# A recurrent layer's weight low parts queued behind the last convolution tap, and the last tile's scans behind a low part

## The chip, the core and the metric

The kernel runs on one core of one Trainium2 chip. The core has five engines, each of which works through a queue of its own strictly in order: TensorE (PE, matrix products; PEld is its weight load), VectorE (DVE), ScalarE (ACT), GpSimd (POOL) and SyncE (SP, which here only issues transfers). An instruction that needs the result of another engine waits at the head of its queue, and everything behind it waits too. The metric is the device time of one execution in microseconds (us). The median of the three runs before is 1522.43 us (1521.42 to 1522.82).

## What is computed

The reference is one inference step of two layers on 640 tokens (512 latent tokens on a grid of 8 x 64, and 128 context tokens), model width 1024. Layer 0 mixes tokens by attention, layer 1 by a linear recurrence in both directions; each is followed by a gated feed-forward part. The change lies in layer 1's mixer:

```python
def _lru_mixer(xm, h0, w_in, conv_w, conv_b, w_a, b_a, w_i, b_i, lam, w_out):
    gate, xr = jnp.split(xm @ w_in, 2, axis=-1)
    xc = _centred_depthwise_conv(xr, conv_w, conv_b).astype(jnp.float32)
    ...
    a_f, b_f = _rglru_coeffs(xc, w_a[0], b_a[0], w_i[0], b_i[0], lam[0])
    a_b, b_b = _rglru_coeffs(xc, w_a[1], b_a[1], w_i[1], b_i[1], lam[1])
    hs_f, hT_f = _linear_scan(a_f, b_f, h0[:, 0], reverse=False)
    hs_b, hT_b = _linear_scan(a_b, b_b, h0[:, 1], reverse=True)
    y = (hs_f + hs_b).astype(xm.dtype) * jax.nn.gelu(gate)
    return y @ w_out, jnp.stack([hT_f, hT_b], axis=1)

def _rglru_coeffs(xc, w_a, b_a, w_i, b_i, lam):
    ...
    r = jax.nn.sigmoid(jnp.einsum('btnk,nkj->btnj', xb, w_a).reshape(B, T, D) + b_a)
    i = jax.nn.sigmoid(jnp.einsum('btnk,nkj->btnj', xb, w_i).reshape(B, T, D) + b_i)
    log_a = -LRU_C * r * jax.nn.softplus(-lam.astype(jnp.float32))
    a = jnp.exp(log_a)
    b = jnp.sqrt(-jnp.expm1(2.0 * log_a)) * (i * xc)
```

The convolution has four taps along the tokens.

## The kernel before

Activations lie with the features on the 128 partitions and the tokens along them, so the width of 1024 makes eight tiles, numbered 0 to 7 here. To keep float32 accuracy on the fast product format, every operand is split into a high part (a rounded copy) and a low part (the rest): `x = xhi + xlo`. A product then takes three matrix products, high by high (L221), high by the activations' low part (L222), and the weight's low part by high (L223). A weight tile of 1024 x 128 is loaded by `unit` twice in the recurrent stage: as it is by a transfer from SP's queue (`raw`), and as its high part by a transfer from POOL's queue (`whi`); DVE computes the low part, `wlo = raw - whi` (L182). Each of the three has three buffers.

A tile's products are made in two chunks of columns, 384 and 256 tokens wide, each 8 x 3 products into one bank of PSUM (`mm`, three banks). The recurrent stage has sixteen such weight tiles: for each of the eight feature tiles an input tile (`lru_xr`, the branch that goes into the convolution) and a gate tile (`lru_gate`, the branch that goes through GeLU).

The work of one feature tile f has four parts:
- `lru_a`: ACT makes the first tap and adds the bias (L1253), DVE the other three taps (L1255), giving `xc`. Four gate products of PE follow (L1265, `gp`, two PSUM buffers; two gates by two directions, each one 512 and one 131 columns wide), and ACT's tanh of each (L1266). DVE multiplies the input gate by `xc` (L1267).
- `lru_b`: ACT's two exponentials (L1277) and two tanh (L1278), a square root (L1279), with table loads where its functions change; DVE's L1273 before it, and L1280 and L1281 behind it.
- `lru_c`: DVE's four scans, two directions by latent and context tokens (L1290), POOL's copies of the final states (L1292), DVE's sums of the two directions (L1297, L1298).
- `lru_d`: DVE multiplies by the gate branch (L1302), ACT casts the high part (L1307), DVE makes the low part (L1309). These are the operands of the output projection.

The loop in `run` goes over steps t = 0 to 9 and writes, in step t: `lru_a` of tile t, the input tile of t + 1, `lru_b` of tile t - 1, `lru_c` of tile t - 2, the gate tile of t - 2 (from step 3 on), `lru_d` of tile t - 2. The order in each engine's queue isn't this order, though. A scheduler in the framework plays the program through on a model of the machine at build time and queues each instruction when the model has it ready. `issue_after` (wrapped as `pin`) adds a constraint: what is written inside it may not be queued ahead of a given instruction on that instruction's engine. It is an order, not a wait. `unit` and `halves` have an argument `after` for that, which only the low part's instruction (L182) obeys.

The input branch has two buffers (`xr0`, `xr1`), so tile t + 1 can be written while tile t is read. The output projection (`project_halves`) begins with five chunks that use the operand tiles 0 to 5 only, and closes them with tiles 6 and 7.

Of the kernel before, what the change touches and what calls it, by code (L numbers as in the profile page):

```python
# [9 lines left out]
F32 = mybir.dt.float32  # L10
F32R = mybir.dt.float32r
AF = mybir.ActivationFunctionType
ALU = mybir.AluOpType
# [4 lines left out]
KT = D // P  # L18
# [15 lines left out]
LW = 643  # L34
# [91 lines left out]
class _Step:  # L126
# [1121 lines left out]
    def lru_a(self, f, lp):  # L1248
        nc, xr = self.nc, self.xrs[f % 2]
        gw = self.t([P, 2, 2, P], F32, "gw", 2, lp)  # L1250
        nc.sync.dma_start(gw, self.i["wg"][f])
        xc = self.t([P, LW], F32, "xc", 2, lp)
        nc.scalar.activation(xc, xr[:, 0:LW], AF.Identity, scale=self.col("cw0", f), bias=self.col("cb", f))  # L1253
        for j in range(1, 4):
            nc.vector.scalar_tensor_tensor(xc, xr[:, j:j + LW], self.col(f"cw{j}", f), xc, ALU.mult, ALU.add)  # L1255

        def lt():
            return self.t([P, 2, LW], F32, "lt", NLT, lp)
        tr, ti = lt(), lt()
        for w, tl in enumerate((tr, ti)):  # L1260
            for d in range(2):
                c = (w * 2 + d) * KT + f
                ps = self.pp.tile([P, 1024], F32, tag="gp", name=self.nm("gp"), bufs=2)
                for s0, s1 in ((0, 512), (512, LW)):
                    nc.tensor.matmul(ps[:, s0:s1], gw[:, w, d], xc[:, s0:s1], start=True, stop=True)  # L1265
                nc.scalar.activation(tl[:, d], ps[:, 0:LW], AF.Tanh, scale=0.5, bias=self.hb[:, c:c + 1])  # L1266
        nc.vector.scalar_tensor_tensor(ti, ti, 1.0, xc[:, None, :].broadcast_to([P, 2, LW]), ALU.add, ALU.mult)  # L1267
        return lt, tr, ti
# [14 lines left out]

    def lru_c(self, f, a, h):
        nc = self.nc
        for d in range(2):
            st = self.st[:, d * KT + f:d * KT + f + 1]
            for sl, init in ((slice(0, NLAT), self.col(f"h{d}", f)), (slice(C0, LW), 0.0)):
                hv, av = [t[:, d, sl] if d == 0 else t[:, d, sl][:, ::-1] for t in (h, a)]
                nc.vector.tensor_tensor_scan(hv, av, hv, init, ALU.mult, ALU.add)  # L1290
            e = LW - 1 if d == 0 else C0
            nc.gpsimd.tensor_copy(st, h[:, d, e:e + 1])  # L1292
        y = a[:, 0, 0:NTOK]
        fn, bn = [h[:, d, 0:NLAT].rearrange("p (r c) -> p c r", r=ROWS) for d in range(2)]
        for c0, c1, q0 in ((56, 64, 0), (0, 56, 64)):
            yv = y[:, q0:q0 + (c1 - c0) * ROWS].rearrange("p (c r) -> p c r", r=ROWS)
            nc.vector.tensor_tensor(yv, fn[:, c0:c1], bn[:, c0:c1], ALU.add)  # L1297
        nc.vector.tensor_tensor(y[:, NLAT:NTOK], h[:, 0, C0:LW], h[:, 1, C0:LW], ALU.add)  # L1298
        return y

    def lru_d(self, f, y, G, yhi, ylo):
        self.nc.vector.tensor_tensor(y, y, G, ALU.mult)  # L1302
        self.split(yhi[:, f], ylo[:, f], y)

    def split(self, hi, lo, v, after=(None, None)):
        with self.pin(after[1]):
            self.nc.scalar.copy(hi, v)  # L1307
        with self.pin(after[0]):
            self.nc.vector.tensor_tensor(lo, v, hi.bitcast(F32), ALU.subtract)  # L1309

    def lru_gate(self, f, hi, lo, lp, after=None):
        nc = self.nc
# [19 lines left out]
    def run(self):  # L1332
        nc, tc, i, o = self.nc, self.tc, self.i, self.o
# [19 lines left out]
        xhi = self.big()  # L1353
        xlo = self.big()
# [43 lines left out]
        xhi = self.big(n=NTOK + 2)  # L1398
        xlo = self.big(n=NTOK + 2)
# [12 lines left out]
        xhi, xlo = self.nh, self.nl  # L1412

        yhi = self.big()
        ylo = self.big()
        with self.phase("lru", at=1) as lp:
            A, B, C, G = {}, {}, {}, {}
            self.xrs = [self.t([P, 648], F32, f"xr{j}", 1, lp) for j in range(2)]
            for xr in self.xrs:
                for a, b in ((0, 2), (514, 517), (645, 648)):  # L1420
                    nc.gpsimd.memset(xr[:, a:b], 0.0)

            def gate(g, after=None):
                G[g], halves = self.lru_gate(g, xhi, xlo, lp, after)
                return halves
            x0, g0, x1 = self.lru_xr(0, xhi, xlo), gate(0, self.sq), self.lru_xr(1, xhi, xlo, self.dg)
            x0[0](pins={3: self.at})
            g0[0](pins={0: self.rr})
            for step in (x1[0], x0[1], g0[1]):
                step()  # L1430
            for t in range(KT + 2):
                if t < KT:
                    A[t] = self.lru_a(t, lp)
                if t + 1 < KT:
                    for step in self.lru_xr(t + 1, xhi, xlo) if t else x1[1:]:
                        step()
                if 0 < t <= KT:
                    B[t - 1] = self.lru_b(t - 1, *A.pop(t - 1))
                if t > 1:
                    C[t - 2] = self.lru_c(t - 2, *B.pop(t - 2))  # L1440
                if t > 2:
                    for step in gate(t - 2):
                        step()
                if t > 1:
                    self.lru_d(t - 2, C.pop(t - 2), G.pop(t - 2), yhi, ylo)
            nc.gpsimd.dma_start(o["nh"], self.st)
        x1, x2 = self.big(n=NTOK + 2), self.big(n=NTOK + 2)
# [33 lines left out]
```

## Time and profile before

| what | value |
|---|---|
| median of three runs | 1522.43 us |
| the profiled execution, whole time | 1522.34 us |
| its span in the trace | 1520.6 us |
| mean granted clock of PE | 0.991 |

The page gives the busy time of each engine. In a trace's row the first number is the start, the second the duration, both in us from the start of the span; then the engine, the line of the code, the operation, and the tiles as out<-in with partitions x columns. A bracket gives the time that the engine sat idle just before and what ended that. PE's rows overlap, since products are pipelined: the distance from one start to the next is what a product costs. A row of a window of time gives for each engine its busy time (and the count of instructions), then the clock that was granted to PE as a share of the full one, the busy share of the transfer engines, and GB/s. The recurrent stage lies between about 855 and 1030 us.

### The profile page before, as it was taken

To read this page: it belongs to the slowest core of one execution; us is meant where nothing else is said; L and a number is where in the kernel's file an instruction comes from. 1 tells how busy PE (TensorE), PEld (TensorE's weight loads), DVE (VectorE), ACT (ScalarE), POOL (GpSimd) and SP (SyncE) were. 2 spreads that over 40 slices of the span, in tenths; PEclk is the share of its full clock that TensorE was granted. 3 is DMA by queue.
4 is the path that set the end of the run, shared out by engine and by line. 5 is a ranking of instruction groups with operands and counts; after the bars stand their busy time and mean duration, and the time that the engine had idled before them with its cause. 6 is when DMAs were issued, how large, how long until landed. Compare 5 with 4: busy or idle time off the path is not lost. (4 is left out here: it accounts for less than half of the span.)

```text
span 1520.6 us, 26091 instructions
## 1 busy us (share of the span) xinstructions
PE 1491.0 (98%) x10359; PEld 1443.9 (95%) x10359; DVE 1062.4 (70%) x2005; ACT 697.9 (46%) x1268; POOL 253.2 (17%) x276
## 2 busy tenths in 40 slices
PE   8999999899999999999999999999999999999997
PEld 6999999899999999999999888899999999999997
DVE  5778998769999987434443769985965656566555
ACT  4576666754332123312321478864634342434243
POOL 0112132100111110000000114220322323222211
PEclk9999999999999999999999999999999999999999
DMA  9545665336566664222222443335342231323211
GB/s 379 165 142 162 188 188 172 117 136 187 179 190 197 207 195 134 62 84 84 65 64 92 145 131 109 119 104 175 97 125 83 71 111 56 100 67 98 70 56 70
DMA packets 72330, 196.65 MB, mean 129 GB/s; under 512 B 8048, under 2 KB 24592, under 8 KB 72080
## 3 DMA queue, kind: packets, MB, share of 16 engines
q1 hardware_dynamic: 57392, 142.32, 29.7%
q0 software_dynamic: 14240, 51.98, 11.2%
q8 instruction: 81, 1.33, 0.4%
q10 hardware_dynamic: 576, 0.68, 0.1%
q14 instruction: 41, 0.34, 0.1%
HBM read 179.48 MB, written 8.92 MB: 124 GB/s over the span
## 5 line engine op out<-in xcount | busy, mean ns | idle before, releaser
L221 PE MATMUL mm<-big,whi 128*128 128x320 f32 (+3 forms) x1233 | 383.7, 313 | 6.5 <-ACT big L1307 5.3
L222 PE MATMUL mm<-big,whi 128*128 128x320 f32 (+3 forms) x1233 | 383.7, 312 | 0.4 <-DVE big L564 0.2
L223 PE MATMUL mm<-big,wlo 128*128 128x320 f32 (+3 forms) x1233 | 383.9, 312 | 0.0
L221 PEld LDWEIGHTS mm<-big,whi 128*128 128x128 f32 x1233 | 232.8, 189 | 9.2 <-ACT big L1307 6.0
L222 PEld LDWEIGHTS mm<-big,whi 128*128 128x128 f32 x1233 | 233.3, 189 | 2.8 <-DVE big L1309 0.7
L223 PEld LDWEIGHTS mm<-big,wlo 128*128 128x128 f32 x1233 | 232.9, 189 | 1.5
L250 DVE SCALAR_TENSOR_TENSOR mprod<-mraw,csb 128x1024 f32<-128x1024 f32 x160 | 195.1, 1219 | 12.3 <-DMA mraw<-in_wm 11.8
L587 DVE SCALAR_TENSOR_TENSOR x<-mm,G,x 128x320 f32<-128x320 f32 (+2 forms) x192 | 77.9, 436 | 83.7 <-PE mm L223 83.5
L180 ACT CAST whi<-raw 128x1024 fp32r<-128x1024 f32 (+1 forms) x71 | 73.9, 1041 | 108.6 <-PE mm L222 62.4
L182 DVE TENSOR_TENSOR wlo<-raw,whi 128x1024 fp32r<-128x1024 f32 (+1 forms) x87 | 106.0, 1219 | 21.6 <-ACT whi L180 12.5
L221 PE MATMUL mm<-big,whx 128*128 128x320 f32 (+3 forms) x348 | 108.3, 311 | 0.0
L223 PE MATMUL mm<-big,wlx 128*128 128x320 f32 (+3 forms) x348 | 108.0, 310 | 0.0
L222 PE MATMUL mm<-big,whx 128*128 128x320 f32 (+3 forms) x348 | 107.8, 310 | 0.0
L246 POOL DMA_DIRECT2D mraw<-in_wm x80 | 43.1, 538 | 364.8 <-DVE mprod L250 270.5
L221 PE MATMUL mx<-big,whi 128*128 128x320 f32 (+3 forms) x287 | 89.4, 311 | 0.0
L223 PE MATMUL mx<-big,wlo 128*128 128x320 f32 (+3 forms) x287 | 89.1, 311 | 0.0
L222 PE MATMUL mx<-big,whi 128*128 128x320 f32 (+3 forms) x287 | 88.9, 310 | 0.0
L221 PE MATMUL mx<-big,whx 128*128 128x320 f32 (+3 forms) x260 | 80.6, 310 | 0.0
L223 PE MATMUL mx<-big,wlx 128*128 128x320 f32 (+3 forms) x260 | 80.5, 310 | 0.0
L180 ACT CAST whx<-raw 128x1024 fp32r<-128x1024 f32 (+1 forms) x40 | 41.1, 1029 | 85.5 <-PE mm L222 47.9
L222 PE MATMUL mx<-big,whx 128*128 128x320 f32 (+3 forms) x260 | 80.3, 309 | 0.0
L1307 ACT CAST whi<-raw 128x1024 fp32r<-128x1024 f32 (+1 forms) x41 | 41.3, 1008 | 73.2 <-PE mm L222 44.9
(347 smaller groups left out, 3721.5 us busy)
## 6 DMA issues: line engine op xcount, KB each, us to landing
raw<-in_gu SPq DMA_DIRECT2D x88, 512.0 KB, 3.5
mraw<-in_wm POOLq DMA_DIRECT2D x80, 512.0 KB, 3.9
raw<-in_dn SPq DMA_DIRECT2D x24, 512.0 KB, 3.6
sw<-in_wm SPq DMA_DIRECT2D x16, 512.0 KB, 10.7
raw<-in_wqk SPq DMA_DIRECT2D x16, 512.0 KB, 5.0
raw<-in_wi SPq DMA_DIRECT2D x16, 512.0 KB, 3.6
whi<-in_wi POOLq DMA_DIRECT2D x16, 512.0 KB, 4.1
raw<-in_dn SPq DMA_DIRECT2D x16, 448.0 KB, 3.3
```

The lines of the kernel that those rows point to most:

```text
L180: nc.scalar.copy(hi, raw)
L182: nc.vector.tensor_tensor(lo, raw, hi.bitcast(F32), ALU.subtract)
L221: nc.tensor.matmul(ps, hi[:, k], xhi[:, k, s], start=(k == 0), stop=False)
L222: nc.tensor.matmul(ps, hi[:, k], xlo[:, k, s], start=False, stop=False)
L223: self.done = nc.tensor.matmul(ps, lo[:, k], xhi[:, k, s], start=False, stop=(k == last)).ins
L246: nc.gpsimd.dma_start(w, self.i["wm"][l * 6 + j - 2, f])
L250: nc.vector.scalar_tensor_tensor(prod, w, 1.0, self.csb[:, s], ALU.mult, ALU.mult, accum_out=out[:, s, f:f + 1])
L587: self.nc.vector.scalar_tensor_tensor(xs, ps[:, a - t0:b - t0], G[:, s, f:f + 1], xs, ALU.mult, ALU.add)
L1307: self.nc.scalar.copy(hi, v)
```

## The change

There are two edits. First, `lru_a` keeps its last tap's instruction as `self.conv`, and the input tile of step t (from step 1 on) and the gate tile of step t (steps 3 to 7) are made with it as `after`: their low parts may not be queued ahead of the last tap of tile t. Second, `split` returns the instruction of the low part, `lru_d` keeps it as `self.low`, and the scans of the last tile (f = 7) may not be queued ahead of it; at that point it is the low part of tile 6.

```diff
         for j in range(1, 4):
-            nc.vector.scalar_tensor_tensor(xc, xr[:, j:j + LW], self.col(f"cw{j}", f), xc, ALU.mult, ALU.add)
+            self.conv = nc.vector.scalar_tensor_tensor(xc, xr[:, j:j + LW], self.col(f"cw{j}", f), xc, ALU.mult, ALU.add).ins
...
     def lru_c(self, f, a, h):
         nc = self.nc
+        pin = self.low if f == KT - 1 else None
...
-                nc.vector.tensor_tensor_scan(hv, av, hv, init, ALU.mult, ALU.add)
+                with self.pin(pin):
+                    nc.vector.tensor_tensor_scan(hv, av, hv, init, ALU.mult, ALU.add)
...
     def lru_d(self, f, y, G, yhi, ylo):
         self.nc.vector.tensor_tensor(y, y, G, ALU.mult)
-        self.split(yhi[:, f], ylo[:, f], y)
+        self.low = self.split(yhi[:, f], ylo[:, f], y)
...
-            self.nc.vector.tensor_tensor(lo, v, hi.bitcast(F32), ALU.subtract)
+            return self.nc.vector.tensor_tensor(lo, v, hi.bitcast(F32), ALU.subtract).ins
...
-                    for step in self.lru_xr(t + 1, xhi, xlo) if t else x1[1:]:
+                    for step in self.lru_xr(t + 1, xhi, xlo, self.conv) if t else x1[1:]:
                         step()
...
                 if t > 2:
-                    for step in gate(t - 2):
+                    for step in gate(t - 2, self.conv if t < KT else None):
                         step()
```

Since the scheduler plays the whole program through again, the order moves on all engines in this stage. The rows below are the queues as built, without times; line numbers behind L1255 are higher by two in the changed kernel (the scans, L1290, become L1292; L1297 and L1298 become L1299 and L1300; L1302 becomes L1304; L1309 becomes L1311).

**DVE, from the last tap of tile 1 to that of tile 2.** `xc_1624` is tile 1's convolution, `xc_1638` tile 2's. `lt_1616` and `lt_1617` belong to tile 0, `lt_1625` and `lt_1626` to tile 1. `wlo_1668` and `wlo_1681` are low parts of weight tiles, `wlo_1647` that of step 2's input tile. Before:

```order
L1255 SCALAR_TENSOR_TENSOR xc_1624_9718<-xr1_1598_9503,cols_1_61,xc_1624_9718 128x643
L1273 TENSOR_SCALAR lt_1616_9670<-lt_1616_9670 128x1286
L1267 SCALAR_TENSOR_TENSOR lt_1617_9671<-lt_1617_9671,xc_1615_9665 128x1286
L1255 SCALAR_TENSOR_TENSOR xc_1638_9813<-xr0_1597_9502,cols_1_61,xc_1638_9813 128x643
L182 TENSOR_TENSOR wlo_1668_10026<-raw_1666_10023,whi_1667_10025 128x1024
L1255 SCALAR_TENSOR_TENSOR xc_1638_9813<-xr0_1597_9502,cols_1_61,xc_1638_9813 128x643 x2
```

And now, from L1280 of tile 0 on:

```order
L1280 SCALAR_TENSOR_TENSOR lt_1616_9670<-lt_1636_9802,lt_1616_9670 128x1286
L1255 SCALAR_TENSOR_TENSOR xc_1638_9813<-xr0_1597_9502,cols_1_61,xc_1638_9813 128x643
L1281 TENSOR_TENSOR lt_1617_9671<-lt_1617_9671,lt_1616_9670 128x1286
L1255 SCALAR_TENSOR_TENSOR xc_1638_9813<-xr0_1597_9502,cols_1_61,xc_1638_9813 128x643
L1292 SCALAR_TENSOR_TENSOR lt_1617_9671<-lt_1636_9802,cols_1_61,lt_1617_9671 128x512
L1292 SCALAR_TENSOR_TENSOR lt_1617_9671<-lt_1636_9802,lt_1617_9671 128x128
L1292 SCALAR_TENSOR_TENSOR lt_1617_9671<-lt_1636_9802,cols_1_61,lt_1617_9671 128x512
L1292 SCALAR_TENSOR_TENSOR lt_1617_9671<-lt_1636_9802,lt_1617_9671 128x128
L1255 SCALAR_TENSOR_TENSOR xc_1638_9813<-xr0_1597_9502,cols_1_61,xc_1638_9813 128x643
L182 TENSOR_TENSOR wlo_1647_9840<-raw_1645_9837,whi_1646_9839 128x1024
```

Tile 2's taps moved from ahead of tile 0's L1280, L1281 and scans to between them, and the input tile's low part, which stood ahead of tile 1's taps, now stands behind tile 2's last.

**ACT, ahead of the first tap of tile 2.** `mm_1634` and `mm_1635` are the two chunks of tile 2's input branch, copied into `xr0`. Before, the copies of the second chunk stood behind the last tanh of tile 0, with the tap behind them:

```order
L1266 ACTIVATE lt_1617_9671<-gp_1620_9680,l_hb_388_2009 128x643
L1266 ACTIVATE lt_1617_9671<-gp_1621_9684,l_hb_388_2009 128x643
L1245 COPY xr0_1597_9502<-mm_1635_9775 128x16x8
L1245 COPY xr0_1597_9502<-mm_1635_9775 128x128
L1253 ACTIVATE xc_1638_9813<-xr0_1597_9502,cols_1_61 128x643
```

Now a step's whole chain stands ahead of it:

```order
L1266 ACTIVATE lt_1626_9724<-gp_1629_9733,l_hb_388_2009 128x643
L1277 ACT_TABLE_LOAD
L1277 ACTIVATE lt_1636_9802<-lt_1616_9670,l_sm4_387_2007 128x643 x2
L1245 COPY xr0_1597_9502<-mm_1634_9748 128x8x8
L1245 COPY xr0_1597_9502<-mm_1634_9748 128x40x8
L1278 ACTIVATE lt_1616_9670<-lt_1616_9670,l_sp2_386_2005 128x643 x2
L1266 ACTIVATE lt_1626_9724<-gp_1630_9737,l_hb_388_2009 128x643
L1245 COPY xr0_1597_9502<-mm_1635_9775 128x16x8
L1245 COPY xr0_1597_9502<-mm_1635_9775 128x128
L1279 ACT_TABLE_LOAD
L1279 ACTIVATE lt_1616_9670<-lt_1616_9670 128x1286
L1253 ACTIVATE xc_1638_9813<-xr0_1597_9502,cols_1_61 128x643
```

Tile 2's first tap moved from behind tile 0's tanh to behind tile 1's tanh and tile 0's square root. In the later steps the same chain stands there, one tile further on.

**PE, ahead of the first gate product of tile 2** (`gp_1641`). `mm_1648` and `mm_1649` are the chunks of step 2's input tile (weights `whi_1646`, `wlo_1647`), `mm_1662` the first chunk of step 3's. Before, the input tile of step 2 was done and the next begun:

```order
L223 MATMUL mm_1649_9870<-big_1512_8886,wlo_1647_9840 128x256
L221 MATMUL mm_1662_9950<-big_1512_8886,whi_1660_9946 128x384
L222 MATMUL mm_1662_9950<-big_1513_8887,whi_1660_9946 128x384
L223 MATMUL mm_1662_9950<-big_1512_8886,wlo_1661_9947 128x384
L221 MATMUL mm_1662_9950<-big_1512_8886,whi_1660_9946 128x384
L1265 MATMUL gp_1641_9820<-xc_1638_9813,gw_1637_9811 128x512
```

Now:

```order
L221 MATMUL mm_1649_9870<-big_1512_8886,whi_1646_9839 128x256
L222 MATMUL mm_1649_9870<-big_1513_8887,whi_1646_9839 128x256
L221 MATMUL mm_1662_9950<-big_1512_8886,whi_1660_9946 128x384
L222 MATMUL mm_1662_9950<-big_1513_8887,whi_1660_9946 128x384
L1265 MATMUL gp_1641_9820<-xc_1638_9813,gw_1637_9811 128x512
L1265 MATMUL gp_1641_9820<-xc_1638_9813,gw_1637_9811 128x131
L1265 MATMUL gp_1642_9824<-xc_1638_9813,gw_1637_9811 128x512
L1265 MATMUL gp_1642_9824<-xc_1638_9813,gw_1637_9811 128x131
L223 MATMUL mm_1648_9843<-big_1512_8886,wlo_1647_9840 128x384
```

All but the first pair of each chunk of step 2's input tile moved behind tile 2's first two gate products. The later steps stand alike: first pairs, the step's first two gate products, most of the input tile's first chunk, the other two gate products among its end, its second chunk, and from step 3 on the gate tile.

At the end of the stage DVE's queue had the scans of tiles 6 and 7 in one piece; now a weight's low part, tile 6's sums, its product with the gate branch and its low part stand between them. Tile 7's sums, product and low part follow its scans.

## The prediction

> **What bounds the kernel now.** I read the page first, then the waits, then the recurrent stage (about 855 to 1030 us) in slices and in order of time.
>
> ```profile
> PE 1491.0 (98%) x10359; PEld 1443.9 (95%) x10359; DVE 1062.4 (70%) x2005; ACT 697.9 (46%) x1268; POOL 253.2 (17%) x276
> ```
>
> TensorE (PE) is busy 98% of the span, so the kernel is bound by it, and time can be won or lost only where PE stands still or runs slowly. In the recurrent stage three of its waits exceed 1 us (times in us; row: start, duration, engine, line; in brackets the idle time before it):
>
> ```profile
> 918.17 1.97 PE L1265 MATMUL gp<-xc,gw 128*128 128x512 f32 x4 [1.85 <-ACT lt L1266]
> 978.92 1.32 PE L1265 MATMUL gp<-xc,gw 128*128 128x512 f32 x4 [1.07 <-issue]
> 1020.09 0.41 PE L221 MATMUL mm<-big,whi 128*128 128x320 f32 x1 [1.63 <-ACT big L1307]
> ```
>
> The second is one that the change touches. VectorE (DVE) had this in its queue just then:
>
> ```profile
> 976.80 1.22 DVE L182 TENSOR_TENSOR wlo<-raw,whi 128x1024 fp32r<-128x1024 f32 x1 [2.11 <-DMA whi<-in_wi]
> 977.94 0.88 DVE L1255 SCALAR_TENSOR_TENSOR xc<-xr,cols,xc 128x643 f32<-128x643 f32 x1
> ```
>
> A weight's low part waited 2.11 us for its transfer, with the last tap of tile 7 queued behind it; the tap ended at 977.94 + 0.88 = 978.82, and PE's gate product came 0.1 us later. After the first and third wait PE also runs at half clock (the number before the DMA share is the granted clock):
>
> ```profile
> 919.00:920.00 1.00, 1.00 (x4) 0.51 (x3) 1.00 (x1) 0.00 (x0) 1.00 (x1) 0.50 0.93 377
> 920.00:921.00 1.00, 1.00 (x5) 1.00 (x5) 1.00 (x3) 0.83 (x2) 1.00 (x1) 0.50 0.15 57
> 921.00:922.00 1.00, 1.00 (x3) 0.65 (x3) 1.00 (x2) 1.00 (x2) 1.00 (x1) 0.50 0.00 0
> 1022.00:1024.00 2.00, 2.00 (x9) 2.00 (x9) 2.00 (x2) 1.07 (x2) 0.00 (x0) 0.50 1.00 391
> ```
>
> Three microseconds at 0.50 lose 1.5 us; I charge that to every long wait. So the most that the stage can give back is 1.85 + 1.07 + 1.63 + 2 x 1.5 = 7.6 us.
>
> **The change, part by part.** No instruction is added or removed; only queue places move. The first edit ties the low parts of step t's weights behind the last tap of tile t. In the order before, the low part for the input tile of step 2 stood ahead of the taps of tile 1, and PE worked one tile ahead. Now that low part stands behind the last tap of tile 2, so PE can do only the first pair of products of each open chunk before it needs it. In PE's order the gate products of tile t (L1265), which need that same tap, come right after those pairs. PE therefore stands at the first gate product until the last tap of tile t has ended. Call that moment T(t). The question is what lies between T(t) and T(t+1), and whether PE has work for that long.
>
> PE's durations: one gate product, then a 384-wide and a 256-wide chunk of 24 products.
>
> ```profile
> 882.05 1.24 PE L1265 MATMUL gp<-xc,gw 128*128 128x512 f32 x4
> 883.05 0.36 PE L223 MATMUL mm<-big,wlo 128*128 128x256 f32 x1
> ...
> 990.39 0.34 PE L221 MATMUL mm<-big,whi 128*128 128x384 f32 x1
> 994.61 0.28 PE L221 MATMUL mm<-big,whi 128*128 128x256 f32 x1
> 997.46 0.31 PE L221 MATMUL mx<-big,whi 128*128 128x320 f32 x1
> ```
>
> A gate product takes 1.00 from start to start, the chunks 4.22 (0.176 a product) and 2.85 (0.119), a whole weight tile 7.07. A step of PE has four gate products, one input tile and, from step 3 on, one gate tile: 4.0 + 7.07 + 7.07 = 18.1 us, without the gate tile 11.1.
>
> ScalarE's (ACT) durations, one after the other without a gap:
>
> ```profile
> 893.14 1.28 ACT L1277 ACT_TABLE_LOAD   x1
> 894.43 1.74 ACT L1277 ACTIVATE lt<-lt,l_sm 128x643 f32<-128x643 f32 x2
> 896.08 0.91 ACT L1278 ACTIVATE lt<-lt,l_sp 128x643 f32<-128x643 f32 x1
> 896.89 0.78 ACT L1266 ACTIVATE lt<-gp,l_hb 128x643 f32<-128x643 f32 x1
> 897.57 0.92 ACT L1278 ACTIVATE lt<-lt,l_sp 128x643 f32<-128x643 f32 x1
> 898.39 0.48 ACT L1245 COPY xr<-mm 128x128 f32<-128x128 f32 x2
> 898.78 0.79 ACT L1266 ACTIVATE lt<-gp,l_hb 128x643 f32<-128x643 f32 x1
> 899.58 1.28 ACT L1279 ACT_TABLE_LOAD   x1
> 900.87 1.28 ACT L1279 ACTIVATE lt<-lt 128x1286 f32<-128x1286 f32 x1
> 902.06 0.91 ACT L1253 ACTIVATE xc<-xr,cols 128x643 f32<-128x643 f32 x1
> ...
> 904.97 0.84 ACT L1245 COPY xr<-mm 128x64 f32<-128x64 f32 x2
> ```
>
> And DVE's:
>
> ```profile
> 961.58 1.50 DVE L1280 SCALAR_TENSOR_TENSOR lt<-lt,lt 128x1286 f32<-128x1286 f32 x1
> 962.99 0.88 DVE L1255 SCALAR_TENSOR_TENSOR xc<-xr,cols,xc 128x643 f32<-128x643 f32 x1
> 963.79 0.82 DVE L1302 TENSOR_TENSOR lt<-lt,gl 128x640 f32<-128x640 f32 x1
> 964.53 1.49 DVE L1281 TENSOR_TENSOR lt<-lt,lt 128x1286 f32<-128x1286 f32 x1
> 965.93 1.22 DVE L182 TENSOR_TENSOR wlo<-raw,whi 128x1024 fp32r<-128x1024 f32 x1
> 967.07 0.82 DVE L1309 TENSOR_TENSOR big<-lt,big 128x640 fp32r<-128x640 f32 x1
> 967.81 1.28 DVE L1290 TENSOR_TENSOR_SCAN lt<-lt,cols,lt 128x512 f32<-128x512 f32 x1
> 969.00 0.40 DVE L1290 TENSOR_TENSOR_SCAN lt<-lt,lt 128x128 f32<-128x128 f32 x1
> 969.32 1.26 DVE L1290 TENSOR_TENSOR_SCAN lt<-lt,cols,lt 128x512 f32<-128x512 f32 x1
> 970.50 0.40 DVE L1290 TENSOR_TENSOR_SCAN lt<-lt,lt 128x128 f32<-128x128 f32 x1
> 970.81 1.21 DVE L1297 TENSOR_TENSOR lt<-lt 128x64 f32<-128x64 f32 x2
> ```
>
> From these I walk the new queues. **One loop, T(t) to T(t+1)**, in the order that the three queues now have:
> - PE: 0.1 to start, two gate products 2.0, half clock 1.5, sixteen products of the input tile's 384 half 2.8, the third gate product 1.0, and 0.24 by which its record outlasts its turn: 7.6.
> - ACT, which takes its queue in order: tanh 0.8, two exponentials 1.65, tanh (L1278) 0.81, the fourth gate's tanh 0.68, the copies of the 384 half 0.84, tanh 0.82, copies of the 256 half 0.48, table load 1.29, square root 1.28: 8.65. PE has finished both halves by the time ACT copies them.
> - DVE: L1280 needs that root and stands ahead of the first tap: 1.41, tap 0.80, L1281 1.40, tap 0.80, four scans 3.00, last tap 0.88: 8.3.
>
> Together 24.6 us, against 18.1 of PE work (19.6 with the half clock): PE idles 5 us or more a step, and long waits bring the half clock each time. In steps 4 to 6 ACT loads one more table ahead of the exponentials (1.29), and in step 4 L1302 stands ahead of the last tap (0.74) and two more products are needed first (0.35): 27.0, 25.9, 25.9.
>
> **The start.** PE begins the input tile of step 1 at 872.59; tile 1's first tap follows ACT's row at 873.39.
>
> ```profile
> 868.64 1.81 DVE L1255 SCALAR_TENSOR_TENSOR xc<-xr,cols,xc 128x643 f32<-128x643 f32 x2 [4.87 <-ACT xc L1253]
> ...
> 872.59 0.34 PE L221 MATMUL mm<-big,whi 128*128 128x384 f32 x1
> ...
> 873.39 0.93 ACT L1253 ACTIVATE xc<-xr,cols 128x643 f32<-128x643 f32 x1
> ```
>
> T(0) = 868.64 + 0.80 + 0.80 + 0.88 = 871.1 and T(1) = 874.3 + 2.5 = 876.8 are early enough. PE: pairs until 873.2, two gate products to 875.2, a pair, two more to 877.5, tile 1's first when its bank is emptied, 877.6 to 878.6, 18 products to 881.8, the next gate product to 882.8, three products, and tile 1's third gate product to 884.3. ACT then has 0.8 + 1.29 + 1.65 + 0.84 + 1.64 + 0.68 + 0.48 + 1.29 + 1.28 = 9.95 from 884.5 to the root's end at 894.5; DVE's 8.3 gives T(2) = 902.8. PE has run dry at about 889: 14 us idle. Then T(3) = 927.4, T(4) = 952.0, T(5) = 979.0, T(6) = 1004.9, T(7) = 1030.8, where before T(7) was 978.8: **+52.0 us**.
>
> What gets better is worth little: the low parts no longer hold the taps (the 1.07 above), and PE's other two waits are inside the new ones.
>
> **The tail.** Behind T(7) PE had 1018.46 - 978.92 = 39.5 us of work; now 0.94 of it (three pairs) lies ahead and 1.5 of half clock is added, so it ends at T(7) + 40.2. The second edit puts the scans of tile 7 behind the low part of tile 6. Before, both tiles' high parts came together at T(7) + 41.3. Now tile 6's comes earlier by four scans and a sum (3.0 + 1.2), but the half clock delays the chain by 1.5: T(7) + 38.6, in time. Tile 7's follows after low part 0.8, scans 3.0, sums 1.4 (estimated from the 1.21 row), product 0.8 and cast 0.8 (taken as the rows of the same width): T(7) + 45.4. PE does tile 6's fifteen products meanwhile (2.2, at an estimated 0.147 for 320 columns, between 0.119 and 0.176) and waits. End before: 41.3 + 30 products 4.4 + half clock 1.5 = T(7) + 47.2; now 45.4 + 2.2 + 1.5 = T(7) + 49.1: **+1.9**. Its bounds: -2.2 if tile 7's part came no later than both did before, since PE has then done tile 6's fifteen; +4.6 if tile 6's comes no earlier than before (41.3 + 6.8 + 2.2 + 1.5 = 51.8).
>
> Sum: 52.0 + 1.9 = 53.9. The profiled execution took 1522.34 us in all, 0.09 below the median of the runs; 1522.3 + 53.9 = **1576 us**.
>
> A rule against this arithmetic: the Trainium skill (ScalarE: Activation LUTs, What ACT_TABLE_LOAD costs) gives a switch of tables 1.28 us for the load and some 1.38 more for a drain. Here the load at 899.58 starts when the row before it ends (898.78 + 0.79), so the trace shows the 1.28 alone. With the drain the ten loads on the path (2, 1, 1, 2, 2, 2) would add 14 us, an estimate from that page: 1590.
>
> **Unknown sizes.** The half clock after waits of 5 to 14 us is not in this trace. Nothing lost: 6 x 1.5 = 9 less, 1567. Clock at 0.50 all the way to the third gate product: the 5.8 us of PE work ahead of that product's end becomes 11.6, 4.3 more than I charge in each of the five loops, 21 in all: 1597. I take the 1.5, seen after two waits.
>
> **Rivals.**
> - *The later steps are covered* (0.08): if ACT and DVE needed only the 7.07 us that PE's gate tile lasts, PE would be the bound from T(3) on: 927.4 + 4 x 18.1 = 999.8, 21 late, 1545 with the tail. Against it: 8.65 + 8.3 is more than twice 7.07, and fixed by the queues.
> - *The loop is dearer* (0.05): the slow clock lasts as long as the bound above allows, 1597. For it: waits of 5 to 14 us are longer than any that the rows above show.
> - *ACT pauses at table loads* (0.02): ten loads on the path, each with a pause as long as itself, add 10 x 1.28 = 13 us: 1589. Against it: the load at 899.58 follows without one.
> - *Faster* (0.06): a single mechanism, the tap freed of the transfer in front of it. If T(2) came before PE runs dry at 889, PE would never wait for a tap, the 1.07 would go, 1521.3, and with the other two waits and their slow clock 1514.8. For it: the 2.11 row. Against it: ACT's in-order queue puts the input tile's copies behind the exponentials, and DVE's puts the tap behind the root.
>
> **How the numbers follow.** My forecast has 0.79; all cases but the last end slower than before. A measurement of this kernel tells about 0.2%, 3 us, from no change. The last rival splits into 0.04 faster and 0.02 the same; slower 0.94. The range takes in both clock bounds, with room below for steps that are partly covered: 1555 to 1597.
>
> **What would show it.** Right: PE waits of 5 to 14 us in front of the first L1265 product of tiles 2 to 7, released by DVE's tap (L1255), each followed by a granted clock of 0.50; taps of a tile about 25 us apart; ACT's root directly ahead of L1253. Wrong: those waits under 2 us, or tap groups 18 us apart. The tail is right if PE's last wait before the output projection lies between tile 6's and tile 7's products.

## The result: 59 us slower

The changed kernel takes 1581.86 us (median of four runs, 1580.06 to 1582.77), the kernel before 1522.62 us in the same comparison (1521.42 to 1522.94): a ratio of 1.0386, with a 95% interval of 1.0372 to 1.0400. The forecast was 1576 us, the range 1555 to 1597. The profiled execution took 1580.06 us, its span is 1578.3 us against 1520.6, 57.7 more; the mean granted clock of PE is 0.976 against 0.991.

### The profile after

From the page of the changed kernel: busy time of the engines; PE's busy tenths and granted clock in 40 slices of the span (39.5 us each); the group of the gate products (busy us and mean ns, then idle time ahead of them).

```profile
PE 1503.6 (95%) x10359; PEld 1448.1 (92%) x10359; DVE 1064.8 (67%) x2005; ACT 697.3 (44%) x1268; POOL 252.1 (16%) x276
...
PE   8999999899999999999999677889999999999997
...
PEclk9999999999999999999999888999999999999999
...
L1265 PE MATMUL gp<-xc,gw 128*128 128x131 f32 (+1 forms) x128 | 50.6, 542 | 39.7 <-DVE xc L1255 39.7
```

These lines give most of the account. PE still makes 10359 products, but is busy 1503.6 us instead of 1491.0: the same products last 12.6 us longer. The other 57.7 - 12.6 = 45.1 us it stands still. Both fall into the 23rd to the 27th slice, where PE's digits drop to 6, 7 and 8 and the clock's to 8: the recurrent stage. And 39.7 us of the standing belong to one line, L1265, and one releaser, DVE's tap (L1255).

The waits of PE in that stage (855 to 1090 us of the changed kernel): engine, tile and line, what it waited for, us in total, times, longest.

```profile
PE gp L1265 <- DVE xc L1255: 39.7, 6, 10.3
PE mm L221 <- ACT xr L1245: 3.9, 4, 2.1
PE mm L221 <- ACT gl L1321: 3.6, 4, 1.1
PE mm L221 <- ACT big L1309: 2.2, 1, 2.2
```

The six waits themselves, in order of time, for tiles 2 to 7 (PE's rows of the timeline, the bracket giving the idle time and its end):

```profile
903.11 3.82 PE L1265 MATMUL gp<-xc,gw 128*128 128x512 f32 x8 [9.96 <-DVE xc L1255]
...
927.57 4.65 PE L1265 MATMUL gp<-xc,gw 128*128 128x512 f32 x8 [10.28 <-DVE xc L1255]
...
953.40 4.12 PE L1265 MATMUL gp<-xc,gw 128*128 128x512 f32 x8 [4.22 <-DVE xc L1255]
...
980.70 4.28 PE L1265 MATMUL gp<-xc,gw 128*128 128x512 f32 x8 [5.57 <-DVE xc L1255]
...
1007.06 4.65 PE L1265 MATMUL gp<-xc,gw 128*128 128x512 f32 x8 [4.83 <-DVE xc L1255]
...
1033.89 4.65 PE L1265 MATMUL gp<-xc,gw 128*128 128x512 f32 x8 [4.83 <-DVE xc L1255]
```

They stand 24.5 to 27.3 us apart. The two gate products (eight instructions) take 3.8 to 4.7 us, at full clock 2.4 (e9 below): the wait is paid a second time in clock. PE's windows around the second wait show it (from:to, length, PE's busy time and instructions, granted clock, share of the transfer engines, GB/s):

```profile
918.00:919.00 1.00, 0.00 (x0) 1.00 0.89 328
919.00:920.00 1.00, 0.00 (x0) 0.80 0.03 8
920.00:922.00 2.00, 0.00 (x0) 0.50 0.00 0
...
928.00:929.00 1.00, 1.00 (x2) 0.50 0.00 0
929.00:930.00 1.00, 1.00 (x4) 0.50 0.76 78
...
932.00:933.00 1.00, 1.00 (x6) 0.50 0.80 328
933.00:934.00 1.00, 1.00 (x7) 0.87 0.30 123
```

The clock falls to 0.50 while PE waits, and stays there for 5.7 us of work after the restart at 927.57 (to about 933.26, since the last row's mean of 0.87 is a quarter at 0.50 and the rest at 1.00).

Why the tap is late is read from the two other queues between T(2) = 902.20 + 0.86 = 903.06 and T(3). ACT:

```profile
910.86 0.80 ACT L1266 ACTIVATE lt<-gp,l_hb 128x643 f32<-128x643 f32 x1 [3.03 <-PE gp L1265]
...
916.62 1.28 ACT L1279 ACT_TABLE_LOAD   x1
917.92 1.27 ACT L1279 ACTIVATE lt<-lt 128x1286 f32<-128x1286 f32 x1
919.10 0.91 ACT L1253 ACTIVATE xc<-xr,cols 128x643 f32<-128x643 f32 x1
```

And DVE:

```profile
902.20 0.86 DVE L1255 SCALAR_TENSOR_TENSOR xc<-xr,cols,xc 128x643 f32<-128x643 f32 x1
...
919.23 1.50 DVE L1280 SCALAR_TENSOR_TENSOR lt<-lt,lt 128x1286 f32<-128x1286 f32 x1 [2.91 <-ACT lt L1279]
920.64 0.88 DVE L1255 SCALAR_TENSOR_TENSOR xc<-xr,cols,xc 128x643 f32<-128x643 f32 x1
...
923.65 1.27 DVE L1292 TENSOR_TENSOR_SCAN lt<-lt,cols,lt 128x512 f32<-128x512 f32 x1
...
926.65 0.86 DVE L1255 SCALAR_TENSOR_TENSOR xc<-xr,cols,xc 128x643 f32<-128x643 f32 x1
```

The third gate's tanh waits for PE until T(2) + 7.80. From there ACT works to the root's end at 919.19 (8.33), and DVE waits for the root and goes through L1280, two taps, L1281 and four scans to the last tap's end at 927.51 (8.32). Three engines take turns; while two of them work, PE runs out of products.

The tail: the casts of tiles 6 and 7 (ACT) and PE's last wait.

```profile
1072.72 0.73 ACT L1309 CAST big<-lt 128x640 fp32r<-128x640 f32 x1 [6.92 <-DVE lt L1304]
1079.55 0.73 ACT L1309 CAST big<-lt 128x640 fp32r<-128x640 f32 x1 [6.10 <-DVE lt L1304]
...
1080.33 0.63 PE L221 MATMUL mm<-big,whi 128*128 128x320 f32 x1 [2.17 <-ACT big L1309]
```

As a mark for the end of the tail I take one pair of evictions of the output projection (L587, DVE), the same one in every kernel. First before, then after:

```profile
1063.11 0.68 DVE L587 SCALAR_TENSOR_TENSOR x<-mx,G,x 128x192 f32<-128x192 f32 x2 [0.32 <-PE mx L223]
```

```profile
1120.80 0.68 DVE L587 SCALAR_TENSOR_TENSOR x<-mx,G,x 128x192 f32<-128x192 f32 x2 [0.32 <-PE mx L223]
```

It comes 57.7 us later, as much as the span is longer: behind it nothing more is lost. From T(7) on it is 86.97 us (1120.80 - 1033.83) where it was 84.29 (1063.11 - 978.82): the tail costs 2.7.

### The profile page after: what moved, and what is told of

Read it like the earlier page. It is cut to its first block, busy times and chain, and to the rows that moved or that the text cites. A ratio compares the mean times of both kernels' runs of the same rounds, so it can differ in the third digit from the quotient of the medians.

```text
span 1578.3 us, 26098 instructions
## 1 busy us (share of the span) xinstructions
PE 1503.6 (95%) x10359; PEld 1448.1 (92%) x10359; DVE 1064.8 (67%) x2005; ACT 697.3 (44%) x1268; POOL 252.1 (16%) x276
## 5 line engine op out<-in xcount | busy, mean ns | idle before, releaser
L221 PE MATMUL mm<-big,whi 128*128 128x320 f32 (+3 forms) x1233 | 384.9, 314 | 13.9 <-ACT big L1309 5.8
L587 DVE SCALAR_TENSOR_TENSOR x<-mm,G,x 128x320 f32<-128x320 f32 (+2 forms) x192 | 77.7, 436 | 84.0 <-PE mm L223 83.9
L180 ACT CAST whi<-raw 128x1024 fp32r<-128x1024 f32 (+1 forms) x71 | 73.9, 1041 | 111.8 <-PE mm L222 62.4
L1265 PE MATMUL gp<-xc,gw 128*128 128x131 f32 (+1 forms) x128 | 50.6, 542 | 39.7 <-DVE xc L1255 39.7
L1265 PEld LDWEIGHTS gp<-xc,gw 128*128 128x128 f32 x128 | 27.3, 236 | 63.2 <-DVE xc L1255 41.8
L223 PE MATMUL mx<-big,wlx 128*128 128x320 f32 (+3 forms) x260 | 80.5, 310 | 0.0
```

What stands on the lines that cost most here:

```text
L180: nc.scalar.copy(hi, raw)
L221: nc.tensor.matmul(ps, hi[:, k], xhi[:, k, s], start=(k == 0), stop=False)
L223: self.done = nc.tensor.matmul(ps, lo[:, k], xhi[:, k, s], start=False, stop=(k == last)).ins
L587: self.nc.vector.scalar_tensor_tensor(xs, ps[:, a - t0:b - t0], G[:, s, f:f + 1], xs, ALU.mult, ALU.add)
```

## The experiments

### Which part of the change costs it: e1, e2, e3, e10

**e1** is the changed kernel without either tie: only the pin of the last tile's scans is left.

```diff
-                    for step in self.lru_xr(t + 1, xhi, xlo, self.conv) if t else x1[1:]:
+                    for step in self.lru_xr(t + 1, xhi, xlo) if t else x1[1:]:
...
-                    for step in gate(t - 2, self.conv if t < KT else None):
+                    for step in gate(t - 2):
```

> The second edit alone: only the scans of tile 7 behind tile 6's low part; the low parts of the weights are tied to nothing. My theory (the first edit carries the whole loss, the second moves only the tail): 1520 to 1527 us, 1524 as the tail was summed. Rival (the pin on the scans is what stalls DVE and with it the output projection): 1540 or more.

Measured: 1524.22 us, ratio 0.9999 (0.9984 to 1.0014). The pin alone does nothing that can be measured.

**e2** is the kernel before with the tie of the input tiles alone (the first line of the diff above, undone; no gate tie, no pin).

> One part of the first edit alone: only the input tile's low part is tied behind the last tap of the step; gate tiles and scans are free. My theory (the loop closes through the input tile: last tap, its products, the copies on ACT, the next tile's taps): within 6 us of the changed kernel, 1574 to 1586, with waits of 4 to 10 us in front of the first gate product of tiles 2 to 6. Rival (the two low parts in a row and the gate tile's tie hold DVE): below 1550.

Measured: 1579.86 us, ratio 1.0358 (1.0338 to 1.0377). One tie carries nearly all of it. Its waits ahead of the gate products of tiles 2 to 6 are 9.90, 10.28, 4.23, 5.56 and 4.83 us, the same as in the changed kernel within 0.1. Ahead of tile 7's there is only 0.49; PE stands in the tail instead, with tiles 6 and 7 cast together:

```profile
1077.42 0.63 PE L221 MATMUL mm<-big,whi 128*128 128x320 f32 x1 [7.93 <-ACT big L1307]
```

**e3** is the tie of the gate tiles alone.

> The other part of the first edit alone: only the gate tile's low part is tied behind the last tap; input tiles and scans are free. My theory (no loop: the gate tile feeds no tap): 1515 to 1535, and no wait over 3 us in front of a gate product. Rival (the gate tie costs as much as the input tie): 1545 or more.

Measured: 1525.53 us, ratio 1.0011 (0.9999 to 1.0024): no change. One wait ahead of a gate product came to 3.43 us, a little over the bound that was set, released by ACT's copies and not by a tap.

**e10** is the changed kernel without its second edit: both ties, no pin.

```diff
-        pin = self.low if f == KT - 1 else None
...
-                with self.pin(pin):
-                    nc.vector.tensor_tensor_scan(hv, av, hv, init, ALU.mult, ALU.add)
+                nc.vector.tensor_tensor_scan(hv, av, hv, init, ALU.mult, ALU.add)
```

> The changed kernel without its second edit: both ties, no pin of the last tile's scans. The order up to T(7) is the same. Theory A (as the prediction's tail has it: without the pin both casts come together, some 2 us later than before, at about T(7) + 43.5, and all thirty products follow them; with the pin tile 6's fifteen are done while tile 7's cast is still to come): end at about T(7) + 43.5 + 4.4 + 1.5 = 49.4 against 46.5 + 2.2 + 1 = 49.7, so the second edit is worth nothing that can be measured, 1579 to 1584, with one wait of 2 to 4 us ahead of tile 6's products. Theory B (the pin takes a long tail wait away, as the 7.9 us of e2 against the 2.2 of the changed kernel suggest): 4 to 6 us slower than the changed kernel, 1585 to 1589.

Measured: 1580.82 us, ratio 1.0385 (1.0372 to 1.0399), the same as the changed kernel. The tail's wait is 1.77 us, a little under what was expected, at T(7) + 44.0 (T(7) = 1038.17); below it the mark of the tail's end:

```profile
1082.18 0.41 PE L221 MATMUL mm<-big,whi 128*128 128x320 f32 x1 [1.77 <-ACT big L1307]
```

```profile
1123.74 0.68 DVE L587 SCALAR_TENSOR_TENSOR x<-mx,G,x 128x192 f32<-128x192 f32 x2 [0.32 <-PE mx L223]
```

With the pin PE waits 2.17 us between tile 6 and tile 7, without it 1.77 us ahead of both. The mark comes at T(7) + 85.57, with the pin at T(7) + 86.97: in these two traces the pin costs 1.4 us, which the whole times can't tell from nothing. A single trace can't either: DVE's order up to T(7) is the same in both, and yet from T(2) to T(7) this one takes 132.58 us, that of the changed kernel 130.77.

### Is the loop what it was taken for: e6, e7

**e6** takes one link out of the loop: in the changed kernel, the scans of all other tiles may not be queued ahead of the step's last tap.

```diff
-        pin = self.low if f == KT - 1 else None
+        pin = self.low if f == KT - 1 else self.conv
```

> The changed kernel, with one edit: the scans of every tile but the last may not be queued ahead of the last tap of the step, so that VectorE makes the four scans (3.0 us) behind that tap and not ahead of it. Theory A (the loop of tanh, exponentials, root, L1280, tap, L1281, tap, scans, tap): each of the six times that a tap is waited for comes 3.0 us earlier, 6 x 3.0 = 18 us: 1564, between 1560 and 1569; the waits ahead of the gate products are about 3 us shorter (7 and 7, then 1 to 2.5). Theory B (the time between taps is set by something else, for instance the transfers of weights or TensorE's own work at the slow clock): less than 6 us, 1576 to 1583.

Measured: 1558.84 us, ratio 1.0226 (1.0205 to 1.0248): 23 us back, somewhat more than the 18 expected. Three of its waits, at tiles 2, 4 and 7:

```profile
900.30 4.65 PE L1265 MATMUL gp<-xc,gw 128*128 128x512 f32 x8 [7.04 <-DVE xc L1255]
...
946.04 2.43 PE L1265 MATMUL gp<-xc,gw 128*128 128x512 f32 x8 [1.35 <-DVE xc L1255]
...
1017.15 3.64 PE L1265 MATMUL gp<-xc,gw 128*128 128x512 f32 x6 [2.58 <-DVE xc L1255]
```

Each is 2.3 to 2.9 us shorter than in the changed kernel. In the trace (spans 1578.3 and 1557.8, 20.5 us apart), T(2) comes 2.8 us earlier, the way from T(2) to T(7) is 13.9 shorter (116.85 against 130.77), and the way from T(7) to the tail's mark 3.7 shorter (83.24): PE waits for no cast in the tail any more. The first two make 16.7 of the 18 expected; the tail was not reckoned. These sums hold other things too: two more turns of L1304 ahead of a tap (0.74 each), and the full clock at tile 4. DVE's own part, from the root's end to the last tap's, shows the scans alone: at tile 3 it falls from 8.32 to 5.46 us. The scans are on the loop, at about their whole length.

**e7** leaves the ties out of steps 1 to 3.

```diff
-                    for step in self.lru_xr(t + 1, xhi, xlo, self.conv) if t else x1[1:]:
+                    for step in self.lru_xr(t + 1, xhi, xlo, self.conv if t > 3 else None) if t else x1[1:]:
...
-                    for step in gate(t - 2, self.conv if t < KT else None):
+                    for step in gate(t - 2, self.conv if 3 < t < KT else None):
```

> The changed kernel with the two ties in the steps from 4 on alone (none in steps 1 to 3). Theory A (every tied step costs the difference of its loop to TensorE's 18.1 us of work): the last tap of tile 4 comes as before, the three loops behind it take the 27.3, 26.4 and 26.8 us that they take in the changed kernel, 80.5 against 54.3, and the tail about 2: 1522 + 26 + 2 = 1550, between 1543 and 1555; no wait over 3 us ahead of the gate products of tiles 2 to 4, waits of 4 to 7 us ahead of those of 5 to 7. Theory B (most of the loss is the first filling, where TensorE was ahead and has to wait for the first time; later steps are mostly covered): 1526 to 1537.

Measured: 1548.67 us, ratio 1.0164 (1.0142 to 1.0187). T(4) = 925.16 (before 925.54), T(7) = 1005.99: the three loops take 80.8 us, as in the changed kernel (80.5). The waits are those of tiles 5 to 7:

```profile
951.19 4.65 PE L1265 MATMUL gp<-xc,gw 128*128 128x512 f32 x8 [5.56 <-DVE xc L1255]
...
978.65 4.65 PE L1265 MATMUL gp<-xc,gw 128*128 128x512 f32 x8 [4.83 <-DVE xc L1255]
...
1006.04 4.22 PE L1265 MATMUL gp<-xc,gw 128*128 128x512 f32 x6 [4.84 <-DVE xc L1255]
```

The loss is paid per tied step, not once at the start.

### What the slow clock is worth: e5, e9

**e5** is the changed kernel with products that nobody reads, so that PE works through most of each wait. They go into a bank of PSUM of another name (`at`), and stand ahead of the first pairs of steps 2 to 7.

```diff
+        last = None
+        if f > 1:
+            z = self.ps("at")
+            for n in range({2: 66, 3: 54, 4: 18}.get(f, 24)):
+                with self.pin(last or self.done):
+                    last = nc.tensor.matmul(z[:, 0:384], self.xw[:, 0, 0:P], self.xw[:, 0, 0:384], start=True, stop=True).ins
...
-                    nc.tensor.matmul(ps[:, s0:s1], gw[:, w, d], xc[:, s0:s1], start=True, stop=True)
+                    with self.pin(last):
+                        nc.tensor.matmul(ps[:, s0:s1], gw[:, w, d], xc[:, s0:s1], start=True, stop=True)
```

> The changed kernel, with products added that nobody reads (66, 54, 18, 24, 24, 24 of 384 columns, ahead of the first pairs of the steps that wait for the taps of tiles 2 to 7), so that TensorE is busy in most of each long wait. All waits for other engines stay. Theory A: the slow clock behind the waits (granted 0.50 for some 24 us, 12 us of lost work) lies on the loop, since the third gate product comes behind it; with a warm clock the changed kernel gets 8 to 15 us shorter, 1567 to 1574 (a product of VectorE, 0.74 each, moves ahead of a tap in some steps, which gives back up to 2). Granted clock near 1.00 at the restarts, idle ahead of the gate products under 1.5 us. Theory B: the loop is set by ScalarE and VectorE alone and the slow products lie beside them: unchanged, 1579 to 1584. Theory C: the added products get in the way: over 1584.

Measured: 1576.28 us, ratio 1.0339 (1.0305 to 1.0372), between the two theories. The run decides nothing: waits of 2.3 to 2.7 us were left (15.3 us in six), and at five of the six the clock fell to 0.50 all the same.

**e9** mends that: more such products, and the input tile's later products pinned behind the third gate product, so that this keeps its place. The lines are against e5.

```diff
-            for n in range({2: 66, 3: 54, 4: 18}.get(f, 24)):
+            for n in range({2: 77, 3: 63, 4: 26, 5: 33}.get(f, 32)):
...
+                if w == 1 and d == 0:
+                    self.g3 = g
...
-                    for step in self.lru_xr(t + 1, xhi, xlo, self.conv) if t else x1[1:]:
-                        step()
+                    for n, step in enumerate(self.lru_xr(t + 1, xhi, xlo, self.conv) if t else x1[1:]):
+                        step(**({"pins": {1 if n else 6: self.g3}} if t > 1 else {}))
```

> Run e5 again, with what spoilt it mended: more products that nobody reads (77, 63, 26, 33, 32, 32), since e5 left waits of 2.3 to 2.7 us that closed the clock all the same, and the third gate product pinned to its place behind some 17 products of the input tile, since in e5 it came behind 18. VectorE's L1304 (0.74) stands ahead of the last tap of tiles 4 to 7 here, in the changed kernel ahead of that of tile 5 alone. Theory A (the slow clock lies on the loop, ahead of the third gate product): the waits ahead of the gate products are under 1.4 us and the granted clock stays above 0.9 there; the tanh of the third gate starts 6.4 to 6.8 us behind T(t), in the changed kernel 7.8 to 9.2; the way from T(2) to T(7) takes 122 to 125 us against 130.8 (without the moved L1304 it would be 2.2 less); whole time 1569 to 1574. Theory B (the loop is ScalarE's and VectorE's alone): T(2) to T(7) 130 to 133, time 1578 to 1584.

Measured: 1569.98 us, ratio 1.0314 (1.0301 to 1.0327), 11.9 us under the changed kernel by the medians. The restart at tile 3, and PE's windows there:

```profile
928.67 2.43 PE L1272 MATMUL gp<-xc,gw 128*128 128x512 f32 x8 [0.63 <-DVE xc L1255]
```

```profile
928.00:929.00 1.00, 0.37 (x2) 1.00 0.00 0
929.00:930.00 1.00, 1.00 (x5) 1.00 0.00 0
```

The two gate products take 2.43 us where they took 4.65, the clock stays at 1.00, and all six waits for the tap sum to 5.7 us. The third gate's tanh starts 6.7 us behind T(3) to T(6), as Theory A has it (behind T(2) 7.6, only 0.2 less than in the changed kernel). T(2) to T(7) takes 125.05 us against 130.77: 5.7 less, with three more turns of L1304 (0.74 each, 2.2) in it; from T(7) to the tail's mark it is 2.5 less (84.50). So the slow clock is worth 5.7 + 2.2 + 2.5 = 10.4 us in these traces. The medians say 11.9, or 14.1 with the 2.2; two traces of one order differ by 1.8 in this stretch (e10 above), so the figure is good to some 2 us either way. The rest of the loss, some 45 us, is there with PE warm: it is the turn-taking itself.

### Further back, and a better place: e4, e8, e11

**e4** has both ties, without the pin, but behind the tap of the tile before.

```diff
+                self.tap = getattr(self, "conv", None)
                 if t < KT:
                     A[t] = self.lru_a(t, lp)
...
-                    for step in self.lru_xr(t + 1, xhi, xlo) if t else x1[1:]:
+                    for step in self.lru_xr(t + 1, xhi, xlo, self.tap) if t else x1[1:]:
...
-                    for step in gate(t - 2):
+                    for step in gate(t - 2, self.tap if t < KT else None):
```

> Both parts of the first edit, but tied behind the last tap of the tile before (tap of tile t-1 in step t), so that an input tile can again be finished while the taps of the present one are still to come; scans free. My theory (what costs is that the loop of 24 to 27 us closes once a tile; with a tile of slack PE's 18 us of work a step bound it): 1515 to 1535. Rival (any tie of low parts to taps costs, by the order that the scheduler then makes): 1550 or more.

Measured: 1531.88 us, ratio 1.0051 (1.0032 to 1.0070). One tile of slack gives back 50 of the 59 us. The largest wait left is in the tail, 7.8 us for the cast of tiles 6 and 7.

**e8** adds the pin of the scans to e4.

> The changed kernel whole, scans' pin too, but the low parts of step t are tied behind the last tap of tile t - 1. Run e4 was the same without the pin of the scans and kept a loss of 8 us, with a wait of 7.8 us for the cast of tiles 6 and 7 in the tail. Theory A (what was left there is that wait, and the pin is what takes it away when a tie stands ahead of it): the tail's wait falls to 1 to 3 us and the time to 1522 to 1528. Theory B (the tie itself still costs it elsewhere): 1530 to 1534 as in e4.

Measured: 1530.80 us, ratio 1.0046 (1.0031 to 1.0060): Theory B, the pin brings nothing. PE's two waits in the tail show why:

```profile
1022.49 0.63 PE L221 MATMUL mm<-big,whi 128*128 128x320 f32 x1 [3.63 <-ACT big L1309]
...
1029.25 0.64 PE L221 MATMUL mm<-big,whi 128*128 128x320 f32 x1 [2.39 <-ACT big L1309]
```

One wait of 7.8 has become two that sum to 6.0, each followed by slow products. What is late is tile 7's chain as a whole: T(7) is 986.95 against 978.82 before, 8.1 later, since DVE still has L1280 ahead of tile 7's taps and waits 3.13 us for the root there.

```profile
976.80 1.50 DVE L1280 SCALAR_TENSOR_TENSOR lt<-lt,lt 128x1286 f32<-128x1286 f32 x1 [3.13 <-ACT lt L1279]
978.21 0.88 DVE L1255 SCALAR_TENSOR_TENSOR xc<-xr,cols,xc 128x643 f32<-128x643 f32 x1
...
986.07 0.88 DVE L1255 SCALAR_TENSOR_TENSOR xc<-xr,cols,xc 128x643 f32<-128x643 f32 x1
```

PE has other products until then, so its gate product waits 0.8 us at most; the delay comes out at the end, where nothing is left to put in between.

**e11** is the kernel before with one tie, of the gate tile of step 8, behind the last tap of tile 7.

```diff
-                    for step in gate(t - 2):
+                    for step in gate(t - 2, self.conv if t == KT else None):
```

> The kernel before with one tie alone: the low part of the gate tile of step 8 behind the last tap of tile 7. In the kernel before this low part waited 2.11 us for its transfer with that tap behind it, and TensorE then 1.07 us for the tap. Theory A: the tap comes some 2 us earlier, the 1.07 goes and nothing else moves: 1521.5, within the measurement's width of the kernel before (ratio 0.9980 to 1.0010), seen in the trace alone. Theory B (what was hidden behind the 1.07 comes forward): 1522.5 to 1526.

Measured: 1520.68 us (12 runs), ratio 0.9990 (0.9981 to 1.0000): 1.8 us better than before by the medians, with an interval from 0.2% better to no change. The trace does what was expected. DVE's rows:

```profile
972.43 2.77 DVE L1255 SCALAR_TENSOR_TENSOR xc<-xr,cols,xc 128x643 f32<-128x643 f32 x3
976.49 1.22 DVE L182 TENSOR_TENSOR wlo<-raw,whi 128x1024 fp32r<-128x1024 f32 x1 [1.29 <-DMA whi<-in_wi]
```

The low part waits for its transfer behind the tap, which ends at 975.20 instead of 978.82, and PE's 1.07 ahead of tile 7's gate product is gone. The stall ahead of the tap was real; the changed kernel's first edit is a way to remove it that costs far more than it is worth.

## Why the prediction was right, and where its sizes were off

**The mechanism** held step by step. The waits stand where they were put, at the first L1265 product of tiles 2 to 7, released by L1255, and each is followed by a clock of 0.50. Three of the six are a little shorter than the 5 us named as the least (4.22, 4.83 and 4.83). The largest is 10.28 us; of the 14 us forecast for the first, 12.8 are there, 9.96 in one piece and 0.76 and 2.09 ahead of it, where the first pairs wait for ACT to empty a bank. The root stands directly ahead of L1253. T(2) was worked out as 902.8 and is 903.06. e6 shows that the scans are in the chain at their whole length, e7 that each tied step costs its own loop.

**The three parts of the loop**, forecast and measured (each read as in the rows of T(2) above):

| loop from | PE, to third tanh | ACT, to root's end | DVE, to next tap | loop |
|---|---|---|---|---|
| T(2) | 7.6: 7.80 | 8.65: 8.33 | 8.3: 8.32 | 24.6: 24.45 |
| T(3) | 7.6: 9.16 | 8.65: 8.36 | 8.3: 8.32 | 24.6: 25.84 |
| T(4) | 7.95: 8.46 | 9.94: 9.78 | 9.04: 9.05 | 27.0: 27.29 |
| T(5) | 7.6: 8.26 | 9.94: 9.78 | 8.3: 8.32 | 25.9: 26.36 |
| T(6) | 7.6: 8.74 | 9.94: 9.78 | 8.3: 8.31 | 25.9: 26.83 |

DVE's part is right to 0.02, ACT's is 0.16 to 0.32 too long (1.1 in all), PE's too short by 4.1 in all. T(7) is 1033.83 where 1030.8 was forecast: +55.0 on before instead of +52.0. ACT's error has the other sign and hides a part of PE's.

**The mis-sized term is the half clock**, "1.5, seen after two waits". From T(3) on, e9's third tanh comes 1.5 to 2.5 us earlier than the changed kernel's, with some 0.3 of other products put ahead of it: about 2 a wait. The clock is back after 2.8 us of work behind the first wait and 5.7 behind the second; the two waits of the trace before, 1.63 and 1.85 us long, were no measure for that. That is some 2.5 of the 4.1; it is not the same in every execution, as e10's loops show. A part of the rest is there at full clock too: 6.7 - 0.3 = 6.4 us in e9, where the sum without the half clock was 6.1. Most of this lies in the two gate products, which take 2.19 us from start to start at tile 3 (928.67 to 930.86) and were reckoned at 2.0; the way from the third product to its tanh is 1.28 there, reckoned 1.24. The outer bound (slow up to the third gate product, 1597) was too pessimistic.

**The tail** came as described: tile 6's cast at T(7) + 39.6 (forecast 38.6), tile 7's at T(7) + 46.5 (45.4), PE's last wait between the products of the two, and 2.7 us in all against 1.9. Both casts are late by 1.0 to 1.1, and the slow clock behind T(7) fits that: it lasts for 5.2 us of work, 2.6 lost where 1.5 was charged. Together 55.0 + 2.7 = 57.7, the difference of the spans; the medians say 59.

**The rivals.** No later step is covered; e7 speaks against that directly. The loop is dearer by the slow clock, but by some 2.5 us instead of 21. ACT doesn't pause at its table loads: that of 916.62 begins at the end of the copy ahead of it (916.13 + 0.48) and the root 1.30 later, and ACT's part is shorter than reckoned without any pause. The drain of some 1.38 us that the Trainium skill (ScalarE: Activation LUTs, What ACT_TABLE_LOAD costs) adds to a switch isn't seen in these rows either. The faster case had its stall rightly placed, as e11 shows, but the ties don't free the tap: they put the root and the scans ahead of it.

## What to carry to other kernels

- A pin that holds back a producer's work for the engine at the bound takes away its lead. The price is the whole loop through the other engines, less the work that the bound has for that long, once per step: walk the queues of a step in turn and compare the sum with that engine's own work. A pin one step further back kept most of the lead and gave back 50 of 59 us.
- Where a wait comes back in every step, reckon the clock as a second cost beside it, from waits as long as those expected.
- To remove a stall ahead of one instruction, tie the one instruction that stalls, not its whole kind. Even that may win little: here 0.2% at most.

## What the runs showed of the hardware

The granted clock falls earlier and more irregularly than the waits before suggested. In the trace before, PE's wait of 1.63 us in the tail is followed by 0.50. The same wait, 1.59 us long, in the profiled execution of e11 is not (windows as above):

```profile
1018.00:1019.00 1.00, 0.70 (x3) 1.00 0.00 0
1019.00:1020.00 1.00, 0.85 (x6) 1.00 0.50 84
```

Nor do longer waits agree. These are two of e5's, at tiles 3 and 4; behind the first the clock falls to 0.50 and the gate products take 4.12 us, behind the second it stays at 1.00 and they take 2.43:

```profile
930.00 4.12 PE L1272 MATMUL gp<-xc,gw 128*128 128x512 f32 x8 [2.43 <-DVE xc L1255]
...
955.88 2.43 PE L1272 MATMUL gp<-xc,gw 128*128 128x512 f32 x8 [2.36 <-DVE xc L1255]
```

Over the 13 traces, between 855 and 1100 us, no wait of up to 1.6 us was followed by 0.50 on its own account (the longest are 1.54 in e1 and 1.59 in e11), and each of 3.6 us and more came with 0.50. Between these it went both ways: behind 1.63 and 1.85 us in the kernel before the clock fell, behind 1.72 in e1 and even 3.43 in e3 it stayed at 1.00. The Trainium skill (TensorE: Matmul & The Clock Gate, Part 1: The HAM clock gate) has a window of about 3.4 us that runs freely, and half rate after an idle one: here 1.63 us was enough, which is less than that rule asks for, while a window that runs freely would fit that like waits end differently. Nor did the clock come back alike: after 2.8 us of work behind a wait of 9.96 us, after 5.7 behind one of 10.28. The first of these ends with this row:

```profile
905.00:906.00 1.00, 1.00 (x4) 0.52 0.83 102
```

What decides it was not tested.
